# A hybrid attention and retention block on one core: compressed probabilities split before their transposes, token tiles in pairs, a last step in pieces, and a new issue order

## The chip, the cores and the metric

The kernel runs on one core of a Trainium2 chip. The metric is the device time of one execution in microseconds (us); a time is the median of several runs. The engines of the core are TensorE (PE, matrix products; its weight loads appear as PEld), VectorE (DVE), ScalarE (ACT), GpSimd (POOL) and SyncE (SP, which issues most DMA transfers here). PE writes its results to eight PSUM banks of 128 x 512 float32; the other data lie in SBUF.

## The reference

One layer, x of 512 tokens by 1024 channels, all in float32. What is computed, cut to its shape (the projection's columns go to fifteen parts):

```python
h = rms_norm(x, norm_pre)
q_n, k_c, v_c, k_s, v_s, k_w, v_w, g_n, z_n, q_r, k_r, v_r, z_r, m_a, m_b = split(h @ w_in)
# mixer A: 8 heads of 64 in 2 groups; compressed, selected and sliding branch
kc, vc = compress_blocks(k_c, ...), compress_blocks(v_c, ...)     # 31 blocks, a GELU layer of 256
p_c = masked_softmax(q @ kc.T * scale);  o_c = p_c @ vc
o_s, o_w = softmax attention over selected blocks, over the window
o_a = g0 * o_c + g1 * o_s + g2 * o_w
y_a = (o_a * silu(z_n)) @ w_nsa_o
# mixer B: retention, 4 heads, keys of 128, values of 256, chunks of 128
y_b = (groupnorm(retention(q_r, k_r, v_r)) * silu(z_r)) @ w_ret_o
merged = sigmoid(m_a) * y_a + sigmoid(m_b) * y_b
y = x + rms_norm(merged @ w_out, norm_post)
```

## The kernel before

**Products.** Every float32 product is made of three PE matmuls on numbers split into a high and a low part (`hi`, `lo`, type fp32r): high x high, low x high, high x low (`mm3`). The normalised input stands transposed as `hTh` and `hTl`, eight k-tiles of 128 channels by 512 tokens.

**Weight blocks.** `w_in` is taken in blocks of 512 columns (names A, C, Q, Z, MA, MB, ZR, QK, VR), and `w_nsa_o` and `w_ret_o` in the blocks NO and RO. SP streams the raw weights by DMA into four buffers. `splitter` makes each k-tile's high part (`whi<-raw`, mostly on ACT, some by a DVE cast) and `split_lo` the low part (`wlo<-raw,whi`, a DVE subtract), into nine slots. Some blocks have more slots, by `MORE` and `MORE2`. A slot comes free when the last token tile has used it. A block then takes four tiles (of tokens, or of features), each of eight k-tiles by three matmuls, 96 matmuls in all. A tile sums up in one of two PSUM banks (ring `ACC`, bank_84 and bank_85); a function named `tail_...` (or `ret`) reads it out on ACT or DVE and goes on with it. `nat` makes such a tile with tokens in the rows, `tra` with features in the rows. The other banks are the rings `PS` (bank_86, bank_87: scores), `PT` (bank_88, bank_89: transposes) and `PO` (bank_90, bank_91: attention outputs).

**Order.** `main` walks over the blocks: A, C, Q, then `PLAN` (Z, MA0, ZR0, QK0, VR0, PAIR, VR1, MB0, NO0, RO0, MA1, NO1, MB1, RO1), then the output product `out_seven`, which needs seven quarter products in place of eight. Between them the attention, the compression and the tails run as coroutines. The class `Order` decides while the program is built: it keeps a guessed time for each engine, and again and again lets the coroutine with the best priority (`PRIOS`) go on whose operands are due by those guesses plus a margin (`MARGINS`); `SOON` and `PSOON` say how many weights ahead a split counts as urgent, `HOLD` and the like hold single steps back. The result is one fixed order of instructions on each engine. At run time an engine takes them strictly in that order and waits at semaphores.

**Compressed branch.** `att_cmp` makes, for each of four token tiles, the scores of eight heads on the compressed blocks, a softmax, and the product with the gate (`s3`, 128 tokens by 8 heads by 32 blocks). Then for each of the two groups: one PE transpose of 128 x 128 (four heads by 32 blocks), and for each of the four heads a copy of a strip of 32 rows by ACT (the high part) and a subtract by DVE from the same bank (the low part), into `pc`, of which PE takes rows 0 to 95 as one operand.

**Last step.** `tail_o` treats the output product by halves of 512 columns (i = 0, 1) of each token tile t: it adds the parts of the seven products where there are several (`plus`), lets ACT make the sum of squares, multiplies by `norm_post` (DVE), and in the second half adds both sums, lets POOL take the power -1/2, and then does x + o * r in two or three pieces (`stt`, DVE), each written out by a DMA from SP.

## Time and profile before

Three runs took 486.65, 487.49 and 485.64 us; the median is 486.65.

| | |
|---|---|
| profiled execution, its own time | 487.29 us |
| its span | 485.5 us |
| mean granted clock of PE | 0.997 |
| DMA, share of 16 engines by its hardware queue of the weights | 42.1% |
| chain that ended last: PE, DVE, DMA, ACT | 68%, 14%, 9%, 4% |

How to read the rows that follow. In a row of the timeline stand the start in us, the duration in us, the engine, the line of the program, the operation, output<-inputs by the program's names, the tile's shape and type, and a count where like instructions follow each other; brackets at the end give the idle time of the engine just before it and what ended it. A group has the sum in us and the mean in ns behind its bar, then the idle time before such instructions. A row of the waits has the engine, the instruction that waited, the one it waited for, and the total in us, the number of times and the longest. Ends of matmuls are modelled, so consecutive matmuls overlap in the rows; their starts are measured. Lines L228, L240, L249, L253, L276 and L282 are helpers through which all ACT operations, DVE tensor operations, DVE scalar operations, fused operations, matmuls and transposes go.

### The profile page before, as it was taken

How to read it: one execution, taken by the hardware profiler on the slowest of the kernel's cores; microseconds unless marked ns; L12 is line 12 of the kernel's file. 1: busy time of each engine (PE TensorE's matmuls, PEld its weight loads, DVE VectorE, ACT ScalarE, POOL GpSimd, SP SyncE). 2: the span in 40 equal slices, each digit the busy share in tenths (PEclk: the TensorE clock that was granted, in tenths of full speed). 3: DMA queues.
4: the chain of work that ended last, by engine and by line, in shares of the span. 5: the costliest groups of instructions: out<-in, count | busy, mean ns of one | idle time of the engine just before them, and what ended most of it. 6: DMA issues, size and time to landing. Idle time of an engine off the chain costs nothing.

```text
span 485.5 us, 7846 instructions
## 1 busy us (share of the span) xinstructions
PE 473.0 (97%) x2666; PEld 420.4 (87%) x2666; DVE 417.8 (86%) x956; ACT 327.6 (67%) x720; POOL 40.8 (8%) x66
## 2 busy tenths in 40 slices
PE   8999999999999998999999999999999999999994
PEld 7898888888888887888888888998889999988883
DVE  6599899898889989998899998877777868889786
ACT  6797678997778898896677767645425535528542
POOL 3103010213000210000100101000000000000010
PEclk9999999999999999999999999999999999999998
DMA  8958999689999699433567763531474725545814
GB/s 315 399 197 257 366 249 309 173 202 253 345 253 225 118 332 268 137 115 124 112 208 263 242 211 93 129 111 43 143 250 134 247 96 177 186 158 174 292 56 173
DMA packets 31080, 98.75 MB, mean 203 GB/s; under 512 B 3136, under 2 KB 6976, under 8 KB 30272
## 3 DMA queue, kind: packets, MB, share of 16 engines
q1 hardware_dynamic: 24576, 70.85, 42.1%
q0 software_dynamic: 6320, 27.26, 23.5%
q8 instruction: 21, 0.34, 0.3%
q10 hardware_dynamic: 144, 0.14, 0.1%
q14 instruction: 19, 0.16, 0.1%
HBM read 93.52 MB, written 31.98 MB: 258 GB/s over the span
## 4 chain that ended last, share of the span: by engine, by line
PE 68%; DVE 14%; DMA 9%; ACT 4%; issue 3%; SPq 1%; DVEq 0%; POOLq 0%; POOL 0%; ACTq 0%
PE bank L276 57%; PE bank L1303 8%; DVE words L240 4%; DVE wlo L240 3%; DVE arena_r L240 3%; PE bank L282 3%; DMA raw<-in_stream_dram 3%; DMA words<-in_rope_r_dram 3%; ACT arena_r L228 2%; DMA words<-in_x_dram 2%; ACT words L228 1%; DMA words<-in_xT_dram 1%; DVE words L253 1%; DVE words L1032 1%; DMA raw<-out 1%
## 5 line engine op out<-in xcount | busy, mean ns | idle before, releaser
L228 ACT ACTIVATE whi<-raw 128x512 fp32r<-128x512 f32 x166 | 99.9, 626 | 48.7 <-PE bank L276 36.1
L240 DVE TENSOR_TENSOR wlo<-raw,whi 128x512 fp32r<-128x512 f32 x182 | 119.3, 686 | 7.2 <-ACT whi L228 6.5
L276 PE MATMUL bank<-whi,hTh 128*128 128x512 f32 x192 | 71.6, 393 | 1.1 <-DVE arena_r L253 0.8
L276 PE MATMUL bank<-wlo,hTh 128*128 128x512 f32 x192 | 69.3, 381 | 1.3 <-DVE wlo L240 1.2
L276 PE MATMUL bank<-whi,hTl 128*128 128x512 f32 x192 | 68.9, 379 | 0.0
L276 PE MATMUL bank<-arena_r 128*128 128x256 f32 (+2 forms) x328 | 68.3, 327 | 0.4 <-ACT arena_r L228 0.2
L240 DVE TENSOR_TENSOR arena_r<-bank,arena_r 128x512 fp32r<-128x512 f32 (+3 forms) x104 | 56.0, 543 | 10.0 <-ACT arena_r L228 8.8
L228 ACT ACTIVATE arena_r<-bank 128x512 fp32r<-128x512 f32 (+3 forms) x104 | 49.0, 476 | 18.8 <-PE bank L282 17.7
L276 PE MATMUL bank<-arena_r,whi 128*128 128x512 f32 (+1 forms) x208 | 61.6, 372 | 0.0
L228 ACT ACTIVATE words<-words,stat 128x128 f32<-128x128 f32 (+3 forms) x115 | 59.4, 550 | 1.8 <-DVE stat L1032 1.6
L276 PEld LDWEIGHTS bank<-arena_r 128*128 128x128 f32 x328 | 51.5, 189 | 6.4 <-DVE arena_r L240 1.3
L276 PEld LDWEIGHTS bank<-arena_r,whi 128*128 128x128 f32 x208 | 39.1, 189 | 5.0
L276 PEld LDWEIGHTS bank<-wlo,hTh 128*128 128x128 f32 x192 | 36.3, 189 | 6.6 <-DVE wlo L240 2.7
L276 PE MATMUL bank<-hTh,whi 128*128 128x512 f32 (+1 forms) x120 | 41.6, 347 | 0.0
L276 PEld LDWEIGHTS bank<-whi,hTh 128*128 128x128 f32 x192 | 36.1, 189 | 5.9 <-DVE arena_r L253 1.0
L276 PE MATMUL bank<-hTh,wlo 128*128 128x512 f32 (+1 forms) x120 | 40.9, 340 | 0.0
L276 PE MATMUL bank<-hTl,whi 128*128 128x512 f32 (+1 forms) x120 | 40.8, 340 | 0.0
L276 PEld LDWEIGHTS bank<-whi,hTl 128*128 128x128 f32 x192 | 36.3, 189 | 5.0
L240 DVE TENSOR_TENSOR words<-bank,words 128x512 f32<-128x512 f32 (+3 forms) x56 | 33.3, 605 | 4.5 <-ACT words L228 2.4
L276 PE MATMUL bank<-arena_r,wlo 128*128 128x512 f32 x96 | 36.4, 379 | 0.0
L282 PEld LDWEIGHTS bank<-identr,shorts 128*128 128x128 f32 x268 | 30.1, 141 | 6.7 <-DVE words L737 0.7
L228 ACT ACTIVATE words<-words 128x512 f32<-128x512 f32 (+3 forms) x47 | 27.2, 583 | 9.3 <-DVE words L253 5.5
(187 smaller groups left out, 917.1 us busy)
## 6 DMA issues: line engine op xcount, KB each, us to landing
raw<-in_stream_dram SPq DMA_DIRECT2D x73, 512.0 KB, 4.8
pair<-in_stream_dram POOLq DMA_DIRECT2D x6, 1024.0 KB, 15.0
t<-in_stream_dram POOLq DMA_DIRECT2D x6, 1024.0 KB, 17.7
out<-in_stream_dram POOLq DMA_DIRECT2D x6, 1024.0 KB, 16.7
words<-in_x_dram SPq DMA_DIRECT2D x8, 512.0 KB, 7.8
raw<-s SPq DMA_DIRECT2D x8, 512.0 KB, 4.1
raw<-pair SPq DMA_DIRECT2D x8, 512.0 KB, 4.6
raw<-t SPq DMA_DIRECT2D x8, 512.0 KB, 4.5
```

What stands on the lines that cost most here:

```text
L228: S.activation(o, i, func, **kw)
L240: (V if e == "dve" else G).tensor_tensor(o, a, b, op=op)
L253: V.scalar_tensor_tensor(o, a, s, b, op0=op0, op1=op1)
L276: T.matmul(ps, a, b, start=start, stop=stop)
L282: T.transpose(ps, a, idn)
L1032: V.tensor_tensor_reduce(pv[:, b, :], sv[:, b, :], maskp[:, 512 - L:512], 1.0, -NEG, OP.add, OP.min, nm[:, b:b + 1])
L1303: T.matmul(ps[m], a, apart(b), start=n in first and s + j == 0, stop=n in last and s + j == 5, skip_group_check=True)
```

## The change

Four edits, and new numbers for the order.

1. `att_cmp` splits `s3` while its tokens are in the rows: one ACT copy makes the high part, one DVE subtract the low one, interleaved in `s2` (8 heads, high and low, 32 blocks). Two transposes for each group and tile (two heads each) then bring high and low rows at once, and two copies of 64 rows by 2 x 128 bring them to `pc`, on ACT or DVE, whichever the guesses prefer.
2. `nat` and `tra` only say how one k-tile's three matmuls look; the new `tiles` walks over a block. It takes two tiles at a time, and where `SKEW` names the block, it does so many k-tiles of the first, then as many of the second, and so on by turns, each in its own bank: Q by 4, RO0 by 2, RO1 by 4, ZR0 by 1. In all others the tiles stay whole.
3. `tail_o` no longer ends with the final operations: a coroutine `tail_p` takes both sums of squares, POOL's power and the pieces of x + o * r, and yields to the order before each piece. Where nothing is added (`plus` absent), the multiplication no longer has to follow the square in the guesses, though both read the same bank.
4. `rope16` gets its engine from `ROPES`, which says DVE throughout, as before.

The numbers: all `MARGINS` and `PRIOS` are new; `SOON` 2 to 3, `PSOON` 6 to 7, `HOLD` 500 to 1000, `MORE` range(12, 20) to range(12, 24).

```diff
+SKEW = {'Q': 4, 'RO0': 2, 'RO1': 4, 'ZR0': 1}
...
+    s2 = words(25, 512, FR).rearrange("p (h s c) -> p h s c", h=8, s=2)
...
+    def tiles(blk, name, order, three, tail):
+        step = SKEW.get(name, blk.nk)
+        for one, two in zip(order[0::2], order[1::2]):
+            ps = {}
+            for k in range(0, blk.nk, step):
+                for t in (one, two):
+                    if not k:
+                        ps[t] = yield from ACC.get()
+                    for kt in range(k, k + step):
+                        yield blk.ready(kt)
+                        yield blk.ready(kt)
+                        e = three(ps[t], t, kt, *blk.views(kt), kt == 0, kt == blk.nk - 1)
+                        if t == order[-1]:
+                            used_up(e)
+                    if k + step == blk.nk:
+                        od.spawn(tail(t, ps[t], e), 1)
...
         e = tt(s3, sm, zc.unsqueeze(2).broadcast_to([P, 8, 32]), OP.mult, e)
+        yield e, "act"
+        e = act(s2[:, :, 0, :], s3, r=e)
+        yield e, "dve"
+        e = sub_split(s2[:, :, 1, :], s3, s2[:, :, 0, :], e)
...
-            ep = tr(pt[:, 0:P], s3[:, g * 4:g * 4 + 4, :].rearrange("p h c -> p (h c)"), ident, e)
+            for j in range(2):
+                h = g * 4 + 2 * j
+                ep = tr(pt[:, j * P:(j + 1) * P].bitcast(FR), s2[:, h:h + 2].rearrange("p h s c -> p (h s c)"), identr, e)
...
-            eh = [act(pc[0:32, j * P:(j + 1) * P], pt[j * 32:j * 32 + 32, 0:P], r=ep) for j in range(4)]
-            yield eh[-1], "dve"
-            for j in range(4):
-                ep = tt(pc[32:64, j * P:(j + 1) * P], pt[j * 32:j * 32 + 32, 0:P], f(pc[0:32, j * P:(j + 1) * P]),
-                        OP.subtract, eh[-1])
+            pv = pc[0:64].rearrange("p (j i c) -> p j i c", j=2, i=2)
+            es = []
+            for i in range(2):
+                es.append(cp_any(pv[:, :, i, :], pt[i * 64:(i + 1) * 64, 0:256].rearrange("p (j c) -> p j c", j=2), ep))
+            ep = max(es)
...
+    def tail_p(t, e):
+        yield od.need(f"sq{t}")
+        yield max(sq[t]), "dve"
+        e = ts(ss2[:, t, 1:2], ss2[:, t, 1:2], ss2[:, t, 0:1], 4e-6, OP.add, OP.add, max(sq[t]))
+        r2 = sp.tile([P, 1], FT, name="rr", tag="rr", bufs=4)
+        er = tt(r2, ss2[:, t, 1:2], nhalf[:, 0:1], OP.pow, e, "pool")
+        od.flags.add(f"pow{t}")
+        yield od.need(f"wr{t}")
         if t > 1:
             yield lambda: len(parts) == 2 * len(loads)
             yield od.need("pow3")
         for a, b in ((0, 512), (512, D)) if t != 1 else ((0, 384), (384, 768), (768, D)):
-            e = stt(OT[t][:, a:b], OT[t][:, a:b], r2, XR[t][:, a:b], OP.mult, OP.add, er)
+            yield max(er, *wr[t]), "dve"
+            stt(OT[t][:, a:b], OT[t][:, a:b], r2, XR[t][:, a:b], OP.mult, OP.add, er)
             DMA.dma_start(out[t * P:(t + 1) * P, a:b], OT[t][:, a:b])
```

Over the whole program PE has 8 transposes more (2655 to 2663 instructions), DVE 958 to 939 instructions, ACT 647 to 626; POOL and SP have as many as before.

What the new order moves, at three places. First PE at the start of block VR1, where the first token tile ends and the second begins (the k-tile is in the number of the weight; `shorts` and `arena_r` are data of the attention and the retention). Before:

```order
L276 MATMUL bank_84<-whi_175,hTh 128x512
L276 MATMUL bank_84<-wlo_176,hTh 128x512
L276 MATMUL bank_84<-whi_175,hTl 128x512
L276 MATMUL bank_86<-arena_r 128x256
L276 MATMUL bank_86<-arena_r 128x128
L276 MATMUL bank_86<-arena_r 128x256
L276 MATMUL bank_86<-arena_r 128x128
L282 MATMUL bank_88<-identr,shorts_512_828 128x128 x4
L276 MATMUL bank_84<-whi_173,hTh 128x512
L276 MATMUL bank_84<-wlo_174,hTh 128x512
L276 MATMUL bank_84<-whi_173,hTl 128x512
```

And of the change:

```order
L278 MATMUL bank_84<-whi_170,hTl 128x512
L278 MATMUL bank_84<-whi_172,hTh 128x512
L278 MATMUL bank_84<-wlo_173,hTh 128x512
L278 MATMUL bank_84<-whi_172,hTl 128x512
L278 MATMUL bank_84<-whi_176,hTh 128x512
L278 MATMUL bank_84<-wlo_177,hTh 128x512
L278 MATMUL bank_84<-whi_176,hTl 128x512
L278 MATMUL bank_85<-whi_174,hTh 128x512
L278 MATMUL bank_85<-wlo_175,hTh 128x512
L278 MATMUL bank_85<-whi_174,hTl 128x512
```

The second tile goes to the other bank, and the small products between the two tiles stand elsewhere. On DVE at the same place, before, with the retention's read of the first tile (`arena_r<-bank_84,rs_191`) and the add from bank_87 that belongs to the last product of PAIR:

```order
L240 TENSOR_TENSOR wlo_176<-raw,whi_175 128x512
L240 TENSOR_TENSOR wlo_178<-raw,whi_177 128x512
L240 TENSOR_TENSOR words_512_128<-words_512_133,words_512_136 128x512
L240 TENSOR_TENSOR words_512_127<-words_512_127,words_512_128 128x4x64 x2
L253 SCALAR_TENSOR_TENSOR arena_r<-bank_84,rs_191,arena_r 128x512
L240 TENSOR_TENSOR arena_r<-words_256_141,arena_r 128x256
L240 TENSOR_TENSOR words_512_133<-bank_87,words_512_115 128x512
```

And of the change, where that add reads bank_86:

```order
L242 TENSOR_TENSOR wlo_183<-raw,whi_182 128x512
L242 TENSOR_TENSOR wlo_167<-raw,whi_166 128x512
L242 TENSOR_TENSOR arena_r<-bank_88,arena_r 128x512
L242 TENSOR_TENSOR words_512_128<-words_512_128,words_512_129 128x4x64 x2
L255 SCALAR_TENSOR_TENSOR words_512_113<-words_512_127,words_512_113 128x512
L242 TENSOR_TENSOR words_512_133<-bank_86,words_512_115 128x512
L242 TENSOR_TENSOR wlo_169<-raw,whi_168 128x512
```

The add no longer stands behind the read of the first tile, but ahead of the next block's splits.

Second, DVE ahead of the weights of block QK0. Before, the strips of the compressed probabilities, then three of the block's first splits, with attention work between:

```order
L240 TENSOR_TENSOR arena_r<-bank_89,arena_r 32x128 x4
L240 TENSOR_TENSOR wlo_166<-raw,whi_165 128x512
L240 TENSOR_TENSOR wlo_168<-raw,whi_167 128x512
L247 TENSOR_SCALAR words_512_115<-words_512_115,stat_1789 128x256
L240 TENSOR_TENSOR words_256_134<-bank_86,cmask 128x256
L240 TENSOR_TENSOR words_256_134<-bank_86,words_256_134 128x256
L980 TENSOR_REDUCE mx<-words_256_134 128x8
L247 TENSOR_SCALAR mx<-mx 128x8
L240 TENSOR_TENSOR words_256_134<-words_256_134,mx 128x256
L240 TENSOR_TENSOR wlo_170<-raw,whi_169 128x512
```

And of the change, the same splits (the names' numbers are one higher):

```order
L259 RECIPROCAL stat_1874<-stat_1874 128x8
L242 TENSOR_TENSOR stat_1874<-stat_1874,gate 128x8
L238 CAST whi_170<-raw 128x512
L242 TENSOR_TENSOR wlo_169<-raw,whi_168 128x512
L242 TENSOR_TENSOR arena_r<-bank_89,arena_r 128x512
L242 TENSOR_TENSOR wlo_171<-raw,whi_170 128x512
L242 TENSOR_TENSOR arena_r<-bank_88,arena_r 128x512
L242 TENSOR_TENSOR wlo_173<-raw,whi_172 128x512
L242 TENSOR_TENSOR wlo_177<-raw,whi_176 128x512
L242 TENSOR_TENSOR wlo_179<-raw,whi_178 128x512
```

`wlo_170<-raw,whi_169` is instruction 448 of DVE before (repeats counted one by one), and its counterpart `wlo_171<-raw,whi_170` is 438; the block's other splits stand 5 to 37 instructions nearer to the start. The strips are gone, and one high part is made on DVE.

Third, the end of DVE's row (t0 is `words_1024_4385` before and `words_1024_4355` after, t1 the next, t2 and t3 the two after those). Before:

```order
L240 TENSOR_TENSOR words_1024_4385<-bank_90,words_1024_119 128x512
L240 TENSOR_TENSOR words_1024_4386<-words_1024_4386,words_1024_119 128x512
L253 SCALAR_TENSOR_TENSOR words_1024_4385<-words_1024_4385,rr,words_1024_4389 128x512 x2
L249 TENSOR_SCALAR ss_200<-ss_200 128x1
L240 TENSOR_TENSOR words_1024_4386<-bank_87,words_1024_119 128x512
L253 SCALAR_TENSOR_TENSOR words_1024_4386<-words_1024_4386,rr,words_1024_4390 128x384 x2
L253 SCALAR_TENSOR_TENSOR words_1024_4386<-words_1024_4386,rr,words_1024_4390 128x256
```

And of the change:

```order
L242 TENSOR_TENSOR words_1024_4355<-bank_91,words_1024_119 128x512
L242 TENSOR_TENSOR words_1024_4356<-words_1024_4356,words_1024_119 128x512
L251 TENSOR_SCALAR ss_201<-ss_201 128x1
L242 TENSOR_TENSOR words_1024_4356<-bank_86,words_1024_119 128x512
L255 SCALAR_TENSOR_TENSOR words_1024_4355<-words_1024_4355,rr,words_1024_4359 128x512 x2
L251 TENSOR_SCALAR ss_201<-ss_201 128x1
L255 SCALAR_TENSOR_TENSOR words_1024_4356<-words_1024_4356,rr,words_1024_4360 128x384 x2
L255 SCALAR_TENSOR_TENSOR words_1024_4356<-words_1024_4356,rr,words_1024_4360 128x256
```

The product of t1's second half with `norm_post` (from bank_87 before, bank_86 after) moves from behind t1's sum (`ss`) to ahead of t0's final steps.

More of the change, by code (lines that the diff above doesn't have):

```diff
@@ L44 @@
 EARLY = 1300
-HOLD = 500
+HOLD = 1000
 OSUMS = (1, 0, 0, 0, 1, 0, 0, 0)
@@ L581, in ready @@
             return parts[i][2] + PE_LAG if i < len(parts) else (lambda: i < len(parts))
-    def nat(blk, t, n, last, lh=None, ll=None, wait=None):
-        ps = yield from ACC.get()
-        lh = lh or (lambda kt: hTh[:, kt, t * P:(t + 1) * P])
-        ll = ll or (lambda kt: hTl[:, kt, t * P:(t + 1) * P])
-        for kt in range(blk.nk):
-            if wait:
-                yield from wait(kt)
-            yield blk.ready(kt)
-            yield blk.ready(kt)
-            wh, wl, r = blk.views(kt)
-            e = mm3(ps[:, :n], lh(kt), ll(kt), apart(wh), apart(wl), kt == 0, kt == blk.nk - 1, r)
-            if last:
-                used_up(e)
-        return ps, e
@@ L599, in tra @@
-    def tra(blk, j, last, mh, ml):
-        ps = yield from ACC.get()
-        for kt in range(blk.nk):
-            yield blk.ready(kt)
-            wh, wl, r = blk.views(kt)
+    def tiles(blk, name, order, three, tail):
[14 more added lines that the diff above has]
+                        od.spawn(tail(t, ps[t], e), 1)
@@ L605, in tra, with nat, three @@
+    def nat(n):
+        def three(ps, t, kt, wh, wl, r, first, last):
+            c = slice(t * P, (t + 1) * P)
+            return mm3(ps[:, :n], hTh[:, kt, c], hTl[:, kt, c], apart(wh), apart(wl), first, last, r)
+        return three
+    def tra(mh, ml):
+        def three(ps, j, kt, wh, wl, r, first, last):
             c = slice(j * P, (j + 1) * P)
-            xh, xl = apart(mh(kt)), apart(ml(kt))
-            mm(ps, wh[:, c], xh, kt == 0, False, r)
+            xh, xl = apart(mh[:, kt, :]), apart(ml[:, kt, :])
+            mm(ps, wh[:, c], xh, first, False, r)
@@ L608, in tra @@
             mm(ps, wh[:, c], xl, False, False)
-            e = mm(ps, wl[:, c], xh, False, kt == blk.nk - 1)
-            if last:
-                used_up(e)
-        return ps, e
-    hT_of = (lambda kt: hTh[:, kt, :]), (lambda kt: hTl[:, kt, :])
+            return mm(ps, wl[:, c], xh, False, last)
+        return three
     x0 = words(50, KD + 256)
@@ L1880, in main @@
         blk = Block(8, 280)
-        for t in range(NT):
-            ps, e = yield from nat(blk, t, 280, t == NT - 1)
-            od.spawn(tail_c(t, ps, e), 1)
+        yield from tiles(blk, "C", range(NT), nat(280), tail_c)
         for i in range(2):
@@ L1889, in main @@
         od.spawn(attention(), 3)
-        for t in reversed(range(NT)):
-            ps, e = yield from nat(blk, t, 512, t == 0)
-            od.spawn(tail_q(t, ps, e), 1)
+        yield from tiles(blk, "Q", range(NT)[::-1], nat(512), tail_q)
         od.spawn(hidden(bank), 1)
@@ L1900, in main @@
                 yield (gar if name == "NO" else gbr)[0] + PE_LAG
-                for ft in range(4):
-                    ps, e = yield from tra(blk, ft, ft == 3, lambda kt: xh[:, kt, :], lambda kt: xl[:, kt, :])
-                    od.spawn((tail_ya if name == "NO" else tail_yb)(i, ft, ps, e), 1)
+                tail = tail_ya if name == "NO" else tail_yb
+                yield from tiles(blk, f"{name}{i}", range(4), tra(xh, xl), lambda t, ps, e: tail(i, t, ps, e))
                 continue
@@ L1913, in main @@
             blk = Block(8, 512)
[L1914 to L1920 removed]
+            tail = {"Z": tail_z, "MA": lambda t, ps, e: tail_m(i, t, ps, e), "MB": lambda t, ps, e: tail_m(i, t + 4, ps, e),
+                    "ZR": lambda t, ps, e: tail_zr(i, t, ps, e), "QK": lambda t, ps, e: tail_qk(i, t, ps, e),
+                    "VR": lambda t, ps, e: ret(i, t, ps, e)}[name]
+            yield from tiles(blk, f"{name}{i}", range(NT), tra(hTh, hTl) if name in ("Z", "MA", "MB") else nat(512), tail)
             if (name, i) == ("VR", 1):
```

57 lines of the change are left out of this document (26 added, 31 removed).

## The prediction

> **What bounds the kernel now.** I read the page's head first, then the waits of TensorE (PE), then the timeline around every place where PE pauses. The head gives the span, the busy shares and, in 40 slices, the granted clock.
>
> ```profile
> span 485.5 us, 7846 instructions
> PE 473.0 (97%) x2666; PEld 420.4 (87%) x2666; DVE 417.8 (86%) x956; ACT 327.6 (67%) x720; POOL 40.8 (8%) x66
> PEclk9999999999999999999999999999999999999998
> ```
>
> PE is busy for 97% of the span at full clock, so the kernel is PE's stream of matmuls, plus pauses in it, plus a tail. The stream has no fat that this change touches; what can be won is the pauses. The waits of PE name five after the start-up (us in total, times, longest):
>
> ```profile
> PE bank L276 <- DVE wlo L240: 1.2, 1, 1.2
> ...
> PE bank L276 <- DVE arena_r L253: 0.8, 1, 0.8
> PE bank L282 <- DVE words L737: 0.5, 1, 0.5
> PE bank L276 <- ACT words L228: 0.5, 1, 0.5
> PE bank L282 <- DVE arena_r L240: 0.4, 1, 0.4
> ```
>
> These are too small, because the end of a matmul is modelled. Starts are better: I take the time from one start to the next, less what that shape usually takes. The largest pause, in QK0:
>
> ```profile
> 183.17 0.38 PE L276 MATMUL bank<-whi,hTh 128*128 128x512 f32 x1
> 183.38 0.38 PE L276 MATMUL bank<-wlo,hTh 128*128 128x512 f32 x1
> ...
> 183.81 0.79 PE L282 MATMUL bank<-identr,shorts 128*128 128x128 f32 x8
> 184.44 0.45 PE L276 MATMUL bank<-whi,hTh 128*128 128x512 f32 x1
> 186.13 0.48 PE L276 MATMUL bank<-wlo,hTh 128*128 128x512 f32 x1 [1.24 <-DVE wlo L240]
> ```
>
> Undisturbed matmuls of 512 columns start 0.21 us apart (183.17 to 183.38), eight transposes take 0.63 (183.81 to 184.44, 0.079 each). From 184.44 to 186.13 are 1.69 us: a pause of 1.47, where the waits say 1.24. Measured in this way, and with the slower step that follows (about 0.1), 16 places stand out by over 0.1 us behind the start-up, 8.0 us together: one in C (.63), two in Q (.29, .63), one in Z (.39), three in the hidden layers (.33, .73, .36), one ahead of ZR0 (.24), three in QK0 (2.06 together), four in VR0 (1.22 together), one in VR1 (1.09). The first and the last:
>
> ```profile
> 27.91 0.28 PE L276 MATMUL bank<-arena_r,hTl 128*128 128x280 f32 x1
> 28.66 0.37 PE L282 MATMUL bank<-identr,shorts 128*128 128x128 f32 x2 [0.47 <-DVE words L737]
> ```
>
> ```profile
> 291.97 0.49 PE L282 MATMUL bank<-identr,shorts 128*128 128x128 f32 x4
> 293.29 0.48 PE L276 MATMUL bank<-whi,hTh 128*128 128x512 f32 x1 [0.82 <-DVE arena_r L253]
> ```
>
> Between the first two starts one matmul of 280 columns (0.12) should pass, and 0.75 do; between the last two four transposes (0.32), and 1.32 do. Behind 293.29 nothing stands out: from there to PE's end, order alone can win nothing. **A perfect order would win 8.0 us, 1.6%.** That is the ceiling, before what the change adds.
>
> **QK0's pause (2.06).** The matmul waits for the low part of a weight, a subtract on VectorE (DVE):
>
> ```profile
> 180.67 1.18 DVE L240 TENSOR_TENSOR arena_r<-bank,arena_r 32x128 fp32r<-32x128 f32 x4
> 181.88 1.29 DVE L240 TENSOR_TENSOR wlo<-raw,whi 128x512 fp32r<-128x512 f32 x2
> ...
> 185.39 0.68 DVE L240 TENSOR_TENSOR wlo<-raw,whi 128x512 fp32r<-128x512 f32 x1
> ```
>
> DVE was busy throughout; the third subtract stood behind attention work and came 1.6 us after its matmul wanted it (186.07 against 184.44). In the new order the same subtract stands 10 rows earlier on DVE, 2.8 us of DVE work by the durations of such rows, while PE has 2.9 us more work ahead of it. The other seven of this block move 5 to 37 rows. The margin goes from -1.6 to about +4 us, so the pause goes, all 2.06. Two parts cause it: ZR0 alternates by single pieces of k between two token tiles, so the first weight slots come free half-way through the block, not three quarters, and the numbers let splits start one weight sooner. Also the four 32x128 subtracts that stood just ahead (1.18) are gone.
>
> **VR1's pause (1.09).** Before, the second token tile needs the bank that the first has just filled, since the other one is still held:
>
> ```profile
> 292.48 0.75 DVE L253 SCALAR_TENSOR_TENSOR arena_r<-bank,rs,arena_r 128x512 fp32r<-128x512 f32 x1 [1.17 <-ACT arena_r L228]
> 293.48 1.02 DVE L240 TENSOR_TENSOR words<-bank,words 128x512 f32<-128x512 f32 x2
> ...
> 294.20 0.69 ACT L228 ACTIVATE words<-bank,rs 128x512 f32<-128x512 f32 x1 [0.87 <-DVE words L240]
> ```
>
> ScalarE (ACT) reads the last product of PAIR out of the other bank only at 294.20, behind the DVE add at 293.48, which is queued behind the very instruction that PE waits for. In the new order that add stands ahead of the block's remaining splits, and the second tile takes bank_85. Gone, 1.09.
>
> **Smaller pauses.** The rs transposes in Q reuse a bank at once:
>
> ```profile
> 53.30 0.29 PE L282 MATMUL bank<-identr,shorts 128*128 128x128 f32 x2
> 54.00 0.62 PE L282 MATMUL bank<-ident,rs 128*128 128x128 f32 x4 [0.41 <-DVE arena_r L240]
> ```
>
> They now come 3.4 us of PE work after the last use of their bank; the pause, .63 with its restart, goes. Q alternates in halves, so weights 4 to 7 are wanted 12 matmuls later (2.6 us): its .29 goes. In C the transposes stand two matmuls later and their copy sooner: .4 of .63. The first in the hidden layers (.33) has 3 us more slack. **Named gains: 2.06 + 1.09 + .63 + .29 + .4 + .33 = 4.8 us.** Of the other 3.2, slacks rise by 2 to 5 us of order distance in most places, but those that wait for ACT to copy the hidden layer out of a bank keep their neighbours; bounds 0 and 3.2, I take half, 1.6. A new order makes new pauses too. Nothing in the trace prices them; from below they are 0, from above the 2.06 that the worst block has now; I take 1.0.
>
> **Compressed probabilities.** Before, each of eight (token tile, group) takes one transpose, then four copies and four subtracts in strips of 32 rows:
>
> ```profile
> L240 DVE TENSOR_TENSOR arena_r<-bank,arena_r 32x128 fp32r<-32x128 f32 x32 | 9.2, 286 | 0.5
> ...
> L228 ACT ACTIVATE arena_r<-bank 32x128 fp32r<-32x128 f32 x32 | 8.6, 268 | 3.3 <-PE bank L282 2.7
> ...
> L228 ACT ACTIVATE words<-bank 128x256 f32<-128x256 f32 x10 | 3.8, 380 | 1.0 <-PE bank L276 0.9
> ...
> L240 DVE TENSOR_TENSOR arena_r<-words,arena_r 128x256 fp32r<-128x256 f32 x18 | 7.5, 419 | 1.1 <-ACT arena_r L228 1.0
> L228 ACT ACTIVATE arena_r<-words 128x256 fp32r<-128x256 f32 x18 | 7.4, 411 | 8.5 <-DVE words L240 8.5
> ```
>
> After, four splits of 128x8x32 (as the 128x256 rows: DVE .419, ACT .411) and 16 copies of 64x2x128, 3 on DVE and 13 on ACT, between .268 and .380; I take .380, the row with the same elements in a row. DVE: -9.2 + 4 x .419 + 3 x .380 = -6.4 us. ACT: -8.6 + 4 x .411 + 13 x .380 = -2.0. Neither is time by itself: both lie beside a saturated PE and buy only the slack used above; if PE waited for DVE all through, the 6.4 would be time. PE gets eight more transposes, 8 x .079 = **+.63, on the path.**
>
> **Alternation.** It adds no matmul and no weight load: the same three per piece, in another order. It does bring the second bank into use sooner: a pair can start only when both banks are read out. In RO0 (pieces of 2) the first bank is done 6 matmuls, 1.3 us, before the next pair wants it, in ZR0 .65 and the heads in between, in RO1 2.6. An eviction of 128x512 is .69 on ACT (294.20), so 0 in RO0 and RO1 and up to .4 in ZR0, inside the 1.0.
>
> **The tail.** DVE works without a gap from 478.47 to the end, behind the last product:
>
> ```profile
> 477.86 0.38 PE L1798 MATMUL bank<-arena_r,hTh 128*128 128x512 f32 x1
> ...
> 478.33 0.60 ACT L228 ACTIVATE rsrow<-bank 128x512 f32<-128x512 f32 x1 [0.51 <-PE bank L1798]
> 478.47 1.41 DVE L253 SCALAR_TENSOR_TENSOR words<-words,rr,words 128x512 f32<-128x512 f32 x2
> ...
> 479.79 0.21 DVE L249 TENSOR_SCALAR ss<-ss 128x1 f32<-128x1 f32 x1
> 479.92 0.68 DVE L240 TENSOR_TENSOR words<-bank,words 128x512 f32<-128x512 f32 x1
> 480.08 0.54 POOL L240 TENSOR_TENSOR rr<-ss,nhalf 128x1 f32<-128x1 f32 x1 [2.14 <-DVE ss L249]
> 480.65 1.54 DVE L253 SCALAR_TENSOR_TENSOR words<-words,rr,words 128x384 f32<-128x384 f32 x3
> ```
>
> Now the last product is hidden under GpSimd's power (480.08 to 480.62). In the new order it stands ahead of tile 0's two final operations, and the small sum behind them with only the three steps after it: from the sum to the first step pass 480.65 - 479.79 = .86, of which the sum is .13, so **.73 is bare**. In the new order the product waits for ACT's square of the same bank (478.33 to about 479.0), when DVE's work ahead of it is through at some 478.5: up to .5 more. What was behind stays (1.54, then 3.3 us until the writes have landed). Bounds .7 and 1.25; I take **+1.1**.
>
> [...]
>
> **Sum.** -4.8 - 1.6 + 1.0 + .63 + 1.1 = -3.7 us. The profiled execution took 487.29 (its span and 1.8 around it), giving 483.6; the median of the three runs is 486.65, .6 lower, giving 483.0. I forecast between them, 483.3.
>
> **Rivals.**
> - *All the pauses go and no new ones come*: -8.0 + .63 + 1.1 = -6.3, 480.4 to 481.0. For it: every slack that I worked out rises. Against it: slacks by order distance leave out semaphores and DMA. 10%.
> - *The pauses only move.* The DVE is the second engine at 86%; splits drawn forward push attention's probabilities back, and PE waits there. If new pauses cost as much as the named gains but 2: -2 + .63 + 1.1, within .5 of before, 486.4. For it: DVE's work shrinks only 6.4 us. Against it: in the order both kinds of margin grow, that of the weights and that of the attention splits. 28%.
> - *Slower*: each weight split drawn forward takes DVE .65 us (1.29 for two) ahead of an attention split for which PE waits. Beside the 32 strips there are 104 - 32 = 72 of these:
>
> ```profile
> L240 DVE TENSOR_TENSOR arena_r<-bank,arena_r 128x512 fp32r<-128x512 f32 (+3 forms) x104 | 56.0, 543 | 10.0 <-ACT arena_r L228 8.8
> ```
>
>   Where its margin is under .65, PE waits for the rest. If 14 of the 72 wait .5 each (7.0) and only the named gains stand, it is -4.8 + .63 + 1.1 + 7.0 = +3.9: 490.6 to 491.2; from 11 of them on it is slower by half a per cent. For it: before, margins of 0.1 to 1.4 us are common there by the same reckoning. Against it: they rise too. 8%.
> - *The change doesn't do what it says*: the alternation is left unused because both banks are never free at once; the order shows bank_84 and bank_85 by turns, so this is out. What it says of the strips is there as well (no 32x128 row is left). 2% for what I misread.
>
> **How the numbers follow.** The forecast and its neighbourhood (481.5 to 485) have 52%, the rivals 10, 28, 8 and 2. The range goes from 481.0, where all pauses go, to 486.6, where they only move; what lies outside is the slower rival, half of the first and the upper edge of the second, some 20% together. A measurement of this kernel can tell half a per cent, 2.4 us of the median, from no change: faster means below 484.2, slower above 489.1. Faster: the first rival and most of the forecast, 60%; the same: the rest of it and the second rival, 33%; slower 7%.
>
> **What would show it.** In the new profile: no wait of PE for wlo in QK0 and none for the eviction in VR1; the page's matmuls x2674; DVE's busy time down by about 6 us; the last matmul's start 4 to 5 us before 477.86; the time from there to the end of the last DVE operation 5.4 in place of 4.3. I am wrong if PE's waits sum as before with new names, if the evictions in RO0 stand in them, or if the tail gets over 2 us longer.

## The result, and the profile after

Fifteen runs of the changed kernel have a median of 488.91 us (486.46 to 492.54), fifteen of the kernel before beside them 486.39 us (485.28 to 488.11). The measured ratio is 1.0063, with a 95% interval of 1.0039 to 1.0087: the change makes the kernel slower by some 0.6% (the medians differ by 2.5 us, the means by 3.1). The forecast was 483.3, in a range of 481.0 to 486.6. The profiled execution took 491.14 us (before 487.29). Of the twelve runs of a1_again below, two (493.84 and 493.03 us) count as slow and stand in none of its numbers.

The head of the profile after:

```profile
span 489.3 us, 7840 instructions
...
PE 473.5 (97%) x2674; PEld 423.4 (87%) x2674; DVE 412.3 (84%) x937; ACT 323.4 (66%) x699; POOL 38.9 (8%) x66
...
PEclk9999999999999999899999999999999999999998
```

PE has its eight more instructions and is as busy as before. DVE has 5.5 us less work, ACT 4.2 less. In the row of the clock a slice in the middle has an 8. The waits of PE behind the start-up:

```profile
PE bank L278 <- ACT arena_r L230: 3.3, 1, 3.3
PE bank L278 <- ACT words L230: 2.0, 2, 1.2
...
PE bank L284 <- ACT rsrow L230: 0.5, 1, 0.5
PE bank L1313 <- DVE arena_r L255: 0.3, 1, 0.3
```

The waits for `wlo` in QK0 and for the eviction in VR1 are gone, and nearly everything else that the forecast wanted gone. Measured from start to start as before, 7.3 of the old 8.0 us have vanished; what stays is the second pause of the hidden layers, .73 before and 1.03 now. But 6.8 us of pauses stand where there were none, and at the three large ones (5.7 us together) PE's releaser is ACT, not DVE. They lie at two places. First PE in QK0, in the timeline:

```profile
199.72 0.46 PE L284 MATMUL bank<-identr,shorts 128*128 128x128 f32 x4
203.43 0.48 PE L278 MATMUL bank<-arena_r,vcs 96*128 96x512 f32 x1 [3.26 <-ACT arena_r L230]
...
204.62 0.63 PE L278 MATMUL bank<-arena_r 128*128 128x256 f32 x2
205.05 0.64 PE L278 MATMUL bank<-whi,hTh 128*128 128x512 f32 x1
205.48 0.63 PE L278 MATMUL bank<-wlo,hTh 128*128 128x512 f32 x1
205.90 0.63 PE L278 MATMUL bank<-whi,hTl 128*128 128x512 f32 x1
```

PE waits 3.4 us for the operand `pc` of the compressed branch (`arena_r`). From 204.6 on, 1.2 us behind the pause, its matmuls start .43 apart, not .21. ACT at the same place:

```profile
197.50 0.60 ACT L230 ACTIVATE arena_r<-bank 128x512 fp32r<-128x512 f32 x1 [0.86 <-PE bank L284]
201.99 0.72 ACT L230 ACTIVATE words<-words,rs 128x512 f32<-128x512 f32 x1 [3.89 <-DMA words<-in_rope_r_dram]
202.61 0.77 ACT L230 ACTIVATE arena_r<-bank 64x256 fp32r<-64x256 f32 x2
```

The two copies into `pc` (202.61) need nothing that is late. They are queued behind ACT's scaling of a rotation table (201.99), which waits 3.89 us for the table's DMA. PE does not need that table soon; DVE's next instruction does and waits 3.50 us too, but in a3 below PE goes on without it. In these rows ACT does not go ahead with the copies while the scaling waits, which costs 3.9 us of ACT's time and 3.4 of PE's.

Why is the table late? The DMA view gives its time from issue to landing; before (from 195 to 201 us):

```profile
words<-in_rope_r_dram SPq DMA_DIRECT2D x1, 256.0 KB, 4.0
```

and after (from 194 to 203 us, with the share of the 16 DMA engines that POOL's own queue takes):

```profile
q0 software_dynamic: 169, 0.63, 34.9%
...
words<-in_rope_r_dram SPq DMA_DIRECT2D x1, 256.0 KB, 6.9
```

And ACT before:

```profile
199.65 0.41 ACT L228 ACTIVATE words<-words 128x256 f32<-128x256 f32 x1
199.96 0.71 ACT L228 ACTIVATE words<-words,rs 128x512 f32<-128x512 f32 x1
```

Before, the same scale stood ahead of the copies into `pc` too, and did not wait: ACT came to it at 199.96, just when the table had landed (195.91 + 4.0). After, ACT is ready for it at 198.10, 1.9 us sooner, and the table lands at 201.9 (195.02 + 6.9), 2.0 us later. So an order that was right by a hair became wrong by 3.9 us. What delays the table is not tested. A transfer of 1 MB on POOL's queue, issued at 180.97 instead of 178.34, lands at 200.6 instead of 199.4, shortly ahead of the table both times; but that queue's share before, 35.7% from 195 to 201 us, is no smaller.

Second, ACT at the end of Q, in the timeline:

```profile
61.50 0.63 ACT L230 ACTIVATE whi<-raw 128x512 fp32r<-128x512 f32 x1 [3.91 <-DMA raw<-in_stream_dram]
62.04 0.58 ACT L230 ACTIVATE rsrow<-bank 128x512 f32<-128x512 f32 x1
62.52 1.18 ACT L230 ACTIVATE arena_r<-bank 64x512 fp32r<-64x512 f32 x2
63.73 0.63 ACT L230 ACTIVATE whi<-raw 128x512 fp32r<-128x512 f32 x1
64.38 0.69 ACT L230 ACTIVATE words<-bank,rs 128x512 f32<-128x512 f32 x1
```

The same pattern: a weight's high part waits 3.91 us for its raw data, and behind it stand the reads of banks (62.04 and 64.38) for which PE pauses at 61.75 (.70) and 63.54 (1.46). The second high part (63.73) waits for nothing by then; it only takes its .63 us ahead of the read at 64.38.

The clock, by windows. The columns are the window, its length, the busy us and instructions of PE, PEld, DVE, ACT and POOL, PE's granted clock, the DMA engines' share and GB/s:

```profile
195.00:199.00 4.00, 4.00 (x26) 3.48 (x25) 3.42 (x9) 1.20 (x2) 0.00 (x0) 1.00 1.04 290
199.00:203.40 4.40, 1.17 (x9) 0.87 (x7) 0.90 (x6) 1.39 (x4) 0.00 (x0) 1.00 0.29 110
203.40:204.60 1.20, 1.17 (x6) 1.09 (x7) 1.17 (x7) 1.15 (x3) 0.00 (x0) 1.00 0.00 0
204.60:208.00 3.40, 3.40 (x10) 2.78 (x10) 3.31 (x12) 3.40 (x15) 0.00 (x0) 0.50 0.24 77
```

For 3.4 us from 204.6 the clock is half. PE counts as busy there, so no wait shows it; it costs 1.7 us.

The tail, DVE's timeline:

```profile
481.69 0.69 DVE L242 TENSOR_TENSOR words<-bank,words 128x512 f32<-128x512 f32 x1 [1.18 <-ACT rsrow L230]
482.30 1.40 DVE L255 SCALAR_TENSOR_TENSOR words<-words,rr,words 128x512 f32<-128x512 f32 x2
483.62 0.21 DVE L251 TENSOR_SCALAR ss<-ss 128x1 f32<-128x1 f32 x1
484.49 1.54 DVE L255 SCALAR_TENSOR_TENSOR words<-words,rr,words 128x384 f32<-128x384 f32 x3 [0.66 <-POOL rr L242]
```

The last product now waits for the square of its bank, the final operations stand behind it, and POOL's power lies bare (.66). From the last matmul's start (480.50) to the end of DVE's work pass 5.53 us, 4.33 before.

**Where the time went**, for the two profiled executions (+3.85): old pauses -7.3, new ones +6.8, the grown one +.3, half clock behind 205 us +1.7, slower steps at the start (4.6 to 6.5 us) +.9, transposes +.6, tail +1.2. That makes +4.2; the rest, -.4, is spread over the stream. The +1.7 and the +.9 differ between executions of one program, and the +.9 is not the change's doing (last section).

### The profile page after: what moved, and what is told of

It reads as the page before. It is cut to its first block, busy times and chain, and to the rows that moved or that the text cites. A ratio compares the mean times of both kernels' runs of the same rounds, so it can differ in the third digit from the quotient of the medians.

```text
span 489.3 us, 7840 instructions
## 1 busy us (share of the span) xinstructions
PE 473.5 (97%) x2674; PEld 423.4 (87%) x2674; DVE 412.3 (84%) x937; ACT 323.4 (66%) x699; POOL 38.9 (8%) x66
## 4 chain that ended last, share of the span: by engine, by line
PE 79%; DVE 8%; DMA 6%; ACT 3%; issue 2%; SPq 0%; DVEq 0%; POOLq 0%; POOL 0%; ACTq 0%
PE bank L278 62%; PE bank L1313 7%; PE bank L1821 7%; DMA raw<-in_stream_dram 4%; PE bank L284 3%; DVE wlo L242 2%; DVE arena_r L242 2%; DMA words<-in_rope_r_dram 1%; ACT words L230 1%; ACT arena_r L230 1%; DVE words L242 1%; DVE words L255 1%; DMA words<-in_x_dram 1%; SPq L668 0%; DVE words L1042 0%
## 5 line engine op out<-in xcount | busy, mean ns | idle before, releaser
L230 ACT ACTIVATE whi<-raw 128x512 fp32r<-128x512 f32 x169 | 102.0, 627 | 48.6 <-PE bank L278 36.5
L278 PE MATMUL bank<-whi,hTh 128*128 128x512 f32 x192 | 72.9, 401 | 0.2 <-ACT hTh L230 0.2
L230 ACT ACTIVATE arena_r<-bank 128x512 fp32r<-128x512 f32 (+3 forms) x85 | 45.5, 541 | 27.4 <-PE bank L284 26.8
L230 ACT ACTIVATE words<-words,stat 128x512 f32<-128x512 f32 (+3 forms) x106 | 55.6, 556 | 2.2 <-DVE stat L1042 2.1
L242 DVE TENSOR_TENSOR arena_r<-bank,arena_r 128x512 fp32r<-128x512 f32 (+2 forms) x72 | 46.8, 656 | 9.0 <-ACT arena_r L230 8.4
L278 PEld LDWEIGHTS bank<-whi,hTh 128*128 128x128 f32 x192 | 37.1, 194 | 4.6 <-ACT hTh L230 0.5
L242 DVE TENSOR_TENSOR words<-words,words 128x256 f32<-128x256 f32 (+5 forms) x66 | 31.2, 484 | 3.0 <-ACT words L230 1.4
```

What stands on the lines that cost most here:

```text
L230: S.activation(o, i, func, **kw)
L242: (V if e == "dve" else G).tensor_tensor(o, a, b, op=op)
L278: T.matmul(ps, a, b, start=start, stop=stop)
```

## The experiments

Theory A, from these rows: ACT takes its instructions strictly in order, three of them stand ahead of urgent ones, and two of these wait for late transfers; the pauses cost what the old ones did, and long ones bring a stretch at half clock as well. Rivals: DVE's splits, the alternation, or the new form of the strips cost the time. A mean clock below is the mean over a kernel's timed runs; the kernel before has .997 in every batch. It counts the stretch behind PE's last matmul too, where half clock costs nothing.

### The same kernel again, and three moves

`a1_again` is the changed kernel itself. `a2_rope_early` loads that rotation table early, into other words:

```diff
+        if (hp, t) == (0, 1):
+            DMA.dma_start(sg0[:, 0:512], rope_r[0, P:2 * P, :])
...
-        DMA.dma_start(rtab, rope_r[i // 4, i % 4 * P:(i % 4 + 1) * P, :])
+        if i != 1:
+            DMA.dma_start(rtab, rope_r[i // 4, i % 4 * P:(i % 4 + 1) * P, :])
```

Those words still held sigmoids of the merge gates, so merge results of one tile are computed from other numbers; the work is the same. `a3_scale_later` lets ACT issue the scale (its call 307) behind the copies into `pc`, and `a4_split_later` issues two high parts later: the first (call 89) behind the three reads at 62.04 and 62.52, the second (call 93) behind the one at 64.38. The first still stands ahead of that last read, other than the expectation of this run has it:

```diff
+LATER = {307: 309}          # a3
+LATER = {89: 92, 93: 94}    # a4
...
-        S.activation(o, i, func, **kw)
+        n = calls[0]
+        calls[0] += 1
+        if n in LATER:
+            held.append((LATER[n], lambda: S.activation(o, i, func, **kw), o.tensor.name))
+        else:
+            S.activation(o, i, func, **kw)
+        for h in [h for h in held if h[0] == n]:
+            h[1]()
```

> The changed kernel once more, as the yardstick for its neighbours on this chip, and a second profile. Theory A (two operations on ACT stand in its queue ahead of work that PE needs, and wait there for a transfer; the time of the transfer varies from run to run): 488 to 489 us, runs again spread over more than the 3 us of the kernel before; the pauses at 62 to 65 us and at 200 us are there again, with other lengths. Theory B (what costs is the granted clock, which was low in the first microseconds and behind 205 us, whatever the order): the start-up's half clock is there again and the time is above 488 without a long pause.

> Only the load of the second retention rotation table is issued sooner, into memory of its own, so that ACT's scaling of it waits for nothing; all engines keep their order. Theory A: the pause of 3.4 us at 200 us goes, and with it the slow clock of the next 2.5 us (1.6): 5.0 us in an execution like the profiled one, 3 to 5 in the median, 484 to 486. Theory B: the slow clock stays where it was; 0 to 1 us. A third reading (PE would meet the same transfer through DVE, which waits for the table too): 1 us or less, with a new wait of PE for DVE at 201.

> The load stays late; only ACT's scaling of that table moves behind the two copies of the compressed probabilities. Theory A, in the strict form that ACT's queue alone matters: as in the run with the early load, 484 to 486. If DVE, whose next instruction reads the scaled table, blocks PE next: PE goes on at 200.3 and stops again within 2 us until about 203; gain 0.3 to 1.5 us, 487.5 to 488.5. Theory B: no change, 488.9.

> Only two ACT operations move: the high parts of two weights of block Z, at 61.5 and 63.7 us, go behind the four reads of banks that stood behind them. Theory A: the pauses at 61.8 (0.70) and 63.5 (1.46) go: 2.1 us less, 486.5 to 487. Rival: Z then waits for these weights itself; the pause only moves to 65 to 68 us and the time stays within 0.5 us of 488.9.

Beside 486.68 us of before:

| | median us | ratio, 95% interval | mean clock |
|---|---|---|---|
| a1_again | 488.43 | 1.0032 (1.0007 to 1.0057) | .9944 |
| a2_rope_early | 487.54 | 1.0013 (.9996 to 1.0030) | .9939 |
| a3_scale_later | 488.86 | 1.0033 (1.0008 to 1.0057) | .9923 |
| a4_split_later | 486.87 | 1.0002 (.9977 to 1.0027) | .9946 |

On this chip the change costs less, 0.3% with an interval that meets the first one's. In its profile each move took away the pause that it was made for, and the medians of a2 and a4 fell by .9 and 1.6 us; their intervals meet a1's, and a2 missed the 484 to 486 that was expected, with 3.0 us of pauses left at 62 to 66 us. With a3's the median did not fall: the pause at 200 us is gone, but the next table did the same thing 30 us on. ACT in a3:

```profile
226.59 0.72 ACT L238 ACTIVATE words<-words,rs 128x512 f32<-128x512 f32 x1 [3.56 <-DMA words<-in_rope_r_dram]
```

PE paused 1.2 us for it at 230.8. And the mean clock fell to .9923. Where, the windows of a2 show, in which only the pauses at 62 to 64 us were left:

```profile
61.00:65.90 4.90, 2.82 (x15) 1.85 (x13) 1.52 (x4) 2.99 (x6) 1.28 (x2) 1.00 1.05 409
65.90:69.30 3.40, 2.84 (x7) 2.28 (x8) 2.94 (x8) 3.34 (x7) 1.10 (x1) 0.51 0.98 236
```

With two pauses of 1.6 and 1.3 us, 1.1 us of matmuls apart, came 3.4 us at half clock, from .5 us ahead of the second one's end; in a3 the same with pauses of .7 and 1.4. The profiled execution of a1, with its pause of 3.4 us at 199.6, had no such stretch. So the moves confirm the places, and the clock needs an experiment of its own (below).

### Both moves, the tail, and one read more

`b1_two_moves` is a4 with the table loaded early, into words that are free (`words(40, 512)`). `b2_and_tail` also puts the last product of t1 back behind t1's sum:

```diff
+            if t == 1 and i == 1:
+                late.append((o, ps, hc))
+                e = od.op("dve", 1.042 * 512 + 69, e)
+            else:
                 e = tt(o, ps, XR[4][:, hc], OP.mult, e)
...
+        if t == 1:
+            lo, lp, lc = late[0]
+            V.tensor_tensor(lo, lp, XR[4][:, lc], op=OP.mult)
```

`c1_hidden_read` is b2 with the read for which PE pauses in the hidden layers issued ahead of an exponential (`LATER` has 125: 126 as well).

> Both moves at once: the rotation table loaded early (now into memory that is free at that time), and the two weight splits behind the four reads of banks. Theory A (ACT's queue behind late transfers, and the slow clock that some long pauses bring): 2.1 for the splits, 3.4 for the table and 1 to 1.6 for the clock from 489.0: 482 to 484.5; mean granted clock back to 0.997. Theory B (the clock is low whatever the pauses): clock at 0.993 to 0.994 as before, 485.5 to 487.

> As the run with both moves, and at the end the product of the second token tile's second half goes back behind that tile's sum, under GpSimd's power. If the tail is the term of the prediction: 0.7 to 1.1 us under the run with both moves. If the writes to memory end the program whatever DVE does: no difference.

> As the run with both moves and the tail, and one ACT operation more is moved: at 85 us the read of the hidden layer's bank goes ahead of an exponential that waits for DVE. Theory A (what PE loses here is work in ACT's queue behind an operation that waits): the pause of 0.93 goes, 0.9 us under 484.7, 483.5 to 484.2. Rival (PE would wait for the same bank through something else, as it did before the change, 0.63): 0.3 us or less.

| | median us | before beside it | ratio, 95% interval | mean clock |
|---|---|---|---|---|
| b1_two_moves | 485.44 | 486.86 | .9970 (.9955 to .9986) | .9958 |
| b2_and_tail | 484.71 | 486.86 | .9949 (.9930 to .9968) | .9966 |
| c1_hidden_read | 483.93 | 486.56 | .9949 (.9928 to .9970) | .9956 |

With two moves on ACT and one transfer the change is 0.3% faster than before instead of slower, and its clock is nearly that of before. It missed the 482 to 484.5 that was expected. Two pauses of the same kind are left in its profile: PE stops for .91 us at 63.2, since the first moved split waits 3.36 us and the last bank read still stands behind it, and for 1.05 us at 228.6, where the next table comes 3.43 us late. ACT in b1 at the first of them:

```profile
62.91 0.63 ACT L236 ACTIVATE whi<-raw 128x512 fp32r<-128x512 f32 x1 [3.36 <-DMA raw<-in_stream_dram]
63.56 0.69 ACT L238 ACTIVATE words<-bank,rs 128x512 f32<-128x512 f32 x1
```

In a4 the same split waited only .67 us, and PE did not stop: how late a transfer comes differs from execution to execution. The tail gives another 0.7 us. The end of DVE's row in b2:

```profile
476.21 1.41 DVE L267 SCALAR_TENSOR_TENSOR words<-words,rr,words 128x512 f32<-128x512 f32 x2 [0.65 <-POOL rr L254]
477.54 0.21 DVE L263 TENSOR_SCALAR ss<-ss 128x1 f32<-128x1 f32 x1
477.66 0.68 DVE L1788 TENSOR_TENSOR words<-bank,words 128x512 f32<-128x512 f32 x1
478.40 1.54 DVE L267 SCALAR_TENSOR_TENSOR words<-words,rr,words 128x384 f32<-128x384 f32 x3
```

The product again hides t1's power, and from the last matmul's start (475.54) to the end of DVE's work pass 4.40 us, about as before (4.33). c1's pause in the hidden layers went, but .9 us of new ones came at 120 us and 1.4 at 229.6: no gain over b2 that the intervals show. **b2 and c1 beat both kernels.**

### One part at a time

`b3_no_pairs` is the changed kernel with `SKEW = {}`, `b4_old_strips` with the old strips in `att_cmp`, `c2_soon_back` with `SOON` 2 and `PSOON` 6. `c3_new_form_alone` is the kernel before with the new `att_cmp`, and no other edit or number.

> The changed kernel with no alternation at all (all blocks tile by tile); the rest of the order then falls out anew. If alternation is what ended QK0's pause, as the prediction has it: a wait for wlo of 1 to 2 us comes back in QK0 or VR0. If the sooner splits alone suffice: none, and the time is set by the new order's own waits on ACT, 485 to 490.

> The changed kernel with the old strips of the compressed probabilities (32 copies and 32 subtracts of 32 rows, one transpose for each group); the rest of the order falls out anew. By the prediction eight transposes less on PE's path (0.63 less), DVE busy 6.4 us more, ACT 2 us more, and a part of the gained margins lost: new waits of PE for DVE of 0 to 2 us. If the new form of this part were the cause of the loss, the time would come back to 486.5 or less with it gone.

> The changed kernel with the two numbers for urgent splits back at 2 and 6; the order falls out anew. If the sooner splits (3 and 7) end the waits for wlo in QK0 and VR0, these come back here, 1 to 2 us in QK0. If they also bring the splits of block Z ahead of the reads of banks on ACT at 61 us, that pause (2.1) goes. Both: 487 to 489. If the other numbers set both: neither.

> The kernel before with only the new form of the compressed probabilities; its old numbers stay, and the order falls out anew. By the prediction: +0.63 for the transposes, and DVE's and ACT's shorter work adds margin: 485.5 to 487.5. If numbers chosen for one program suit no other, as the changed kernel with the old strips (506.9) hints: several us slower, with new waits of PE on ACT or DVE.

| | median us | before beside it | ratio, 95% interval |
|---|---|---|---|
| b3_no_pairs | 486.71 | 486.86 | .9997 (.9980 to 1.0013) |
| b4_old_strips | 506.88 | 486.86 | 1.0401 (1.0370 to 1.0431) |
| c2_soon_back | 493.11 | 486.56 | 1.0140 (1.0110 to 1.0169) |
| c3_new_form_alone | 489.82 | 486.56 | 1.0063 (1.0041 to 1.0085) |

Three of the four are slower than either kernel or as slow as the changed one, and their waits lie in new places. The waits of c2:

```profile
PE bank L278 <- ACT words L230: 5.8, 4, 2.3
```

and of c3:

```profile
PE bank L276 <- DVE wlo L240: 1.4, 3, 0.8
PE bank L276 <- ACT words L228: 1.3, 2, 0.8
```

In b4, c2 and c3 code and numbers that were not chosen together meet, and each of these runs reorders everything. So undoing a part measures a misfit too, and not the part: the strips alone are not worth 4%. Two things can still be read. b3, without alternation, has neither pause at 62 to 64 nor at 200 us; alternation was no gain here, and without it ACT met the late transfers at other times. (c2 lacks both pauses too, and waits 5.8 us at four other places.) And QK0's old pause is absent in b3, and in c2 with the old `SOON`, while c3 with the old numbers still waits for `wlo`: neither the alternation nor `SOON` is needed to remove it. No run keeps the new numbers and leaves out both, so what does remove it is not settled.

### Pauses put into the kernel before

`d1_pause`, `d2_pause_3` and `d3_pause_1` are the kernel before with one pause at the start of RO1, where it has none: 15, 9 and 4 copies in all.

```diff
+                if (name, i) == ("RO", 1):
+                    bank = PT.free[0][1]
+                    T.transpose(bank[:, 0:P].bitcast(FR), identr, identr)
+                    S.activation(dummy, bank[:, 0:P], AF.Copy)
+                    for _ in range(CHAIN):
+                        S.activation(dummy, f(dummy), AF.Copy)
+                    T.transpose(bank[:, 0:P].bitcast(FR), dummy, identr)
```

> The kernel before with one pause of PE put in, and nothing else: at the start of RO1 (about 421 us, where before has no pause) PE makes a transpose into a free bank, ACT copies it 15 times within a dummy tile, and PE's next transpose waits for the last copy. The pause should be 3 to 4 us long, like the one at 200 us in the changed kernel, and no row of the old order moves otherwise. Theory A, that a pause of such a length makes PE run at half its rate for about 3.4 us behind it in a part of the executions: the time rises by more than the pause, 3.5 + up to 1.7, so 488.5 to 492, the mean granted clock over the runs falls from .997 to .994 to .996, and where the profiled run was hit, steps of .43 us stand behind 425. Rival, that the lower clock of the changed kernel has nothing to do with its pauses: the clock stays at .997 and the time rises by the pause alone, 489.5 to 490.5 at a pause of 3.5. A second rival, that PE's stream has slack there and catches up: under 488.

> As d1_pause with 9 copies in place of 15. There the copies took .34 each and the pause was 5.3, longer than planned; here it should be 3.2 to 3.4 us, the length of the changed kernel's longest. d1_pause lost 8.3 in the median for 5.3 of pause, at a mean clock of .990. Theory A, that pauses shorter than the 3.4 us of one half-rate stretch bring it in part of the executions: mean clock .992 to .996 with runs of both kinds, single runs at .990 to .993 and others at .997, time 3.3 + 0.4 to 2.5 above before. Rival, that only a pause longer than 3.4 us brings it: clock .997 in all runs, time 3.3 above before.

> As d1_pause with 4 copies: a pause of 1.5 to 1.7 us, the length of the pauses that kernel before has. Theory A, with a chance that grows with the length: mean clock .995 to .997, time 1.6 + 0 to 1 above before. Rival, that the half rate has nothing to do with a pause's length: the same clock as in d2_pause_3.

The pauses are from the start of one transpose to the other's, less .08. The loss by the clock is the fall of the mean clock times some 488 us; it is an upper bound, since half clock within the pause costs nothing.

| | pause us | median, above before | ratio, 95% interval | mean clock (before) | loss by the clock |
|---|---|---|---|---|---|
| d1_pause | 5.3 | 494.13, +8.3 | 1.0169 (1.0133 to 1.0206) | .9900 (.9970) | 3.4 |
| d2_pause_3 | 3.2 | 491.26, +4.6 | 1.0080 (1.0053 to 1.0108) | .9933 (.9972) | 1.9 |
| d3_pause_1 | 1.5 | 488.64, +1.9 | 1.0031 (1.0011 to 1.0050) | .9965 (.9972) | .3 |

The windows from the pause on, of d1:

```profile
424.70:428.10 3.40, 3.33 (x9) 2.71 (x10) 2.69 (x7) 2.00 (x6) 0.00 (x0) 0.51 0.95 351
428.10:440.00 11.90, 11.90 (x57) 10.42 (x56) 7.00 (x15) 2.47 (x6) 0.00 (x0) 1.00 0.04 17
```

of d2:

```profile
422.00:425.60 3.60, 0.56 (x6) 0.38 (x4) 2.22 (x4) 3.07 (x11) 0.00 (x0) 1.00 0.60 165
425.60:429.00 3.40, 3.34 (x9) 2.71 (x10) 2.69 (x7) 2.00 (x6) 0.00 (x0) 0.52 0.85 295
```

and of d3:

```profile
423.00:425.20 2.20, 0.81 (x8) 0.63 (x7) 1.99 (x4) 1.82 (x6) 0.00 (x0) 1.00 0.41 123
425.20:428.60 3.40, 3.40 (x17) 3.00 (x18) 3.21 (x8) 2.11 (x5) 0.00 (x0) 1.00 0.77 270
```

Behind 5.3 and 3.2 us PE runs 3.4 us at half clock; behind 1.5 it does not. Over the runs, all six of d1 have a clock of .989 to .992; of d2's six four have .992 or .993 and two .995 and .996, within what before shows; d3's twelve have .995 to .998. So a pause does bring the slow clock, more often the longer it is, and one of the changed kernel's length costs up to half as much again as it lasts. d1's pause came out longer than planned, so its expectation of 3.5 us does not apply, and at 5.3 us it loses more than one stretch accounts for; what the rest is, the profile doesn't show. Both rivals, a clock that has nothing to do with the pauses and a PE that catches up, are out.

## Why the prediction was wrong

- **PE's stream with pauses and a tail bounds the kernel**: right before and after. The pauses measured from start to start were the right measure, and each new wait is in them.
- **Old pauses, -4.8 and -1.6.** They gave more, -7.3. For QK0 the prediction named the alternation and `SOON` as causes; b3 and c2 show that neither alone is needed.
- **New pauses, +1.0. This is the step that failed**: they measured 6.8, and 7.1 with the growth of the one that stayed. The upper bound, 2.06, was taken from the worst block of the kernel before, and that bounds nothing about another order. The margins were counted in rows of DVE and PE, so neither ACT's queue nor the landing of a transfer stood in them. The prediction says itself, against its first rival, that slacks by order distance leave out DMA, and gives that no term. A look at ACT's row for instructions that wait for a DMA ahead of bank reads would have shown the scale of the table at 199.96, free by a hair. b1 settles that this is the cause: with one table early and two splits later the kernel goes from slower to faster than before, though two pauses of the kind are left in it.
- **The clock** stood nowhere in the sum: it was taken as full throughout. The new pauses are longer than the old, and d2 shows what one of 3.2 us does. Over the runs the clock fell from .997 to .9935. Times 488 us that is 1.7 us, but a part of it lies behind PE's last matmul, where the change made the tail longer: in the profiles the clock is half from 482.39 to the end before (3.1 us) and from 484.51 after (4.8 us). b1 and b3 have the same tail, and their profiled runs have a clock of .996 and .995, about what the tail's 4.8 us at half clock take off by themselves (2.4 of 489.3, .005); their means are .9958 and .9949. Against these the clock cost some .7 to 1.1 us of the 2.5, an estimate from the means.
- **Compressed probabilities.** PE +.63 as forecast (x2674). DVE's busy time fell by 5.5 (forecast 6.4), ACT's by 4.2 (2.0); neither was time by itself.
- **Alternation**: no wait for evictions in RO0, ZR0 or RO1, as forecast. That it also shifts when ACT meets a late transfer (b3) was not seen.
- **Tail, +1.1**: 1.2 in the profile, .7 between the medians of b1 and b2. Right in kind: DVE waits 1.18 us for the square of its bank, as forecast.
- **Rivals.** The one in which the pauses only move came nearest in kind: 7.3 against 7.1. The prediction's own sign of being wrong, waits of PE that sum as before with new names, came true, and the last matmul started 2.6 us later than before, not 4 to 5 sooner. The slower rival had the direction, but the wrong engine: its price was DVE's time for weight splits, and no wait of PE for such a split is left.

With the terms measured in the two profiles the prediction's sum is -7.3 + 7.1 + .6 + 1.2 = +1.6 without the clock, and with .7 to 1.1 for it +2.3 to +2.7, where the medians differ by 2.5 and the means by 3.1.

## What to carry to other kernels

On an engine that stands at an instruction that waits, as ACT did for 3.9 us at 201.99 with two copies ready behind it, look in its row for each instruction that waits for a transfer and ask who stands behind it: something needed late that waits for a DMA, ahead of a read that frees a bank, is a pause waiting for its day. When work is reordered, count margins to the landing of the transfers as well, and check each engine that PE waits for, not only the busiest. And price a pause of PE like those that were hit here (3.2 and 3.4 us alone, .7 and 1.4 us or 1.6 and 1.3 us close together) at some 1.7 us more than its length whenever it is hit, for the 3.4 us at half clock behind it.

## What the hardware showed that was not expected

A stretch of half clock lasts 3.4 us behind each of these pauses: 204.6 to 208.0 in the changed kernel, 65.9 to 69.3 in a2, 425.6 to 429.0 in d2. In the profiles of the two kernels the clock changes only at whole multiples of 3.413 us from its first record: before at 4.52 and 482.39 us, 0 and 140 of them on, in the changed kernel at 6.64, 204.62, 208.03 and 484.51 us, 0, 58, 59 and 140 of them on. The pause can be shorter than that: d2's is 3.2 us, and in a2 pauses of 1.6 and 1.3 us with matmuls between them were enough.

The table has stretches of 3.413 us, counted back from a change of the clock, with the time for which PE was idle in each, by starts, as the pauses were measured:

| | stretch, us | PE idle in it, us | clock behind it |
|---|---|---|---|
| the kernel before | 291.24 to 294.65 | 1.1 | full |
| the changed kernel | 197.79 to 201.20 | 1.2 | full |
| the changed kernel | 61.25 to 64.67 | 1.6 | full |
| d1_pause | 417.8 to 421.2 | 1.7 | full |
| a3_scale_later | 61.76 to 65.17 | 2.1 | half |
| the changed kernel | 201.20 to 204.62 | 2.3 | half |
| a2_rope_early | 62.55 to 65.96 | 2.5 | half |
| d2_pause_3 | 422.30 to 425.72 | 3.2 | half |
| d1_pause | 421.2 to 424.6 | 3.4 | half |

In the table the clock is half behind 2.1 us or more and full behind 1.7 us or less. That this idle time is what decides is the author's reading; no run moved a pause of one length against these stretches. It would fit a1 and the changed kernel, one program with one pause of 3.4 us: in the changed kernel 1.2 us of the pause lie ahead of 201.20 and 2.2 behind it, while a1, with full clock from 195 to 212 us, would have had its pause cut nearer the middle, which is not shown. By the clocks of the runs d2's pause of 3.2 us was hit in four of six, and d3's of 1.5 us in none of twelve.

At the start, from 4.6 to 6.5 us, steps of some .4 us show half the rate in some profiled executions (the changed kernel, a1, b1, b3, with 5 matmuls from 4 to 6 us each; not before, a2, b2, with 8, 8 and 7), while the granted clock of that window reads 1.00. The clock's records begin only where these steps end, at 6.64 us in the changed kernel and at 4.52 before, so the mean clock leaves this loss out. It goes by the execution and not by the order: before, d1, d2 and d3 have the same order of instructions until some 420 us, and PE does 39, 39, 36 and 26 matmuls in their first 10 us.
